# Weight pieces of 1024 columns for the high and low parts of an encoder's weights, on rings of four

## The chip, the cores and the metric

The kernel runs on one core of a Trainium2 chip. The metric is the device time of one execution in microseconds (us): the median of three runs. One more execution was recorded by the hardware profiler, and it has a time of its own. The profiler's names for the engines are PE (TensorE, the matrix engine; PEld is its loading of the stationary operand), DVE (VectorE), ACT (ScalarE), POOL (GpSimd) and SP (SyncE, which here only starts transfers).

## What is computed

An encoder trunk of two layers on 512 tokens of 1024 channels, all in fp32. Each layer modulates its input with a vector worked out from `c`, projects it with `w_in` into queries, keys, values and gates, runs two kinds of attention side by side, merges and projects them with `w_out`, and then sends each token through two of 16 experts:

```python
def _moe(h, w_router, router_bias, w_gate, w_up, w_down):
    ...
    hg = jnp.einsum('td,edf->tef', t, w_gate)
    hu = jnp.einsum('td,edf->tef', t, w_up)
    act = jax.nn.silu(hg) * hu * combine[..., None].astype(t.dtype)
    y = jnp.einsum('tef,efd->td', act, w_down)
    return y.reshape(b, s, d)

def reference(x, c, w_ada, ...):
    for l in range(DEPTH):
        ...
        h = _layer_norm(x) * (1.0 + sc1) + sh1
        mix = _mixer(h, w_in[l], ...)
        x = _layer_norm(DN_ALPHA * x + g1 * mix, ln1_g[l], ln1_b[l])
        h = _layer_norm(x) * (1.0 + sc2) + sh2
        ffn = _moe(h, w_router, router_bias, w_exp_gate[l], w_exp_up[l], w_exp_down[l])
        x = _layer_norm(DN_ALPHA * x + g2 * ffn, ln2_g[l], ln2_b[l])
    return x
```

An expert's gate and up weights are 1024 x 256, its down weights 256 x 1024. The kernel computes an expert only for the tokens that chose it, up to 128 of them.

## The kernel before

**Splitting the weights.** Nearly all products with weights are made from three matmuls in a faster 32-bit format. An operand is split into a high part, its value rounded to that format (`wH`, `xH`, `eH`), and a low part, what is left of it (`wL`, `xL`, `eL`); high x high, high x low and low x high are added up in PSUM (`gemm3`, lines 220 to 227). For weights this is done by `wsplit` (line 197). `wraw` (line 187) loads a tile of up to 8 KB for each partition as it lies in memory: 128 rows x 8 row blocks x 256 columns for `w_in`, gate and up, 128 x 2 x 1024 for down. `wsplit` then cuts it into pieces of 512 columns (`h` row blocks), and makes for each piece the high part by a cast on ScalarE (line 215) and the low part by a subtraction on VectorE (line 216).

**Where the tiles lie.** The raw tiles come from a ring of four (`NRAW`, tag `raw`) and one of five (`NE8`, tag `e8`); some that are loaded ahead of the experts lie in free tiles of other pools (`f4`, `row`, in blocks of 1024 columns). `WPAT` says which ring each expert's tile takes. The high and the low parts have rings of six pieces of 2 KB each (`NWH`). A slot comes free when its last reader is done, and the next piece takes any slot that is free.

**The order of the work.** Every engine runs its instructions in a fixed order. A scheduler lays it down when the program is built, from the program's order, the dependences and the time at which it reckons each slot to be free. So a change in the size or number of the slots moves instructions on all engines, though no line that orders them is touched.

**The experts.** For each expert `e` the program issues `x_gate(e)`, `x_down(e - 1)`, `x_up(e)`, `x_split(e + 1)`. `x_load` fetches the 128 tokens of an expert (`xe`, by an indirect transfer on POOL's queue). `x_split` transposes them on TensorE (tile `tp`) and splits them in two halves of 512 columns, row blocks 0 to 3 and 4 to 7, into `xH` and `xL`. `x_gate` and `x_up` are 24 matmuls each; the silu of the gate product and its product with the up product are `ea`. `x_down` transposes `ea` (`eT`), splits it (`eH`, `eL`) and multiplies it with the down weights: the columns 0 to 511 of `w_down` in plain fp32 with `eT`, the columns 512 to 1023 split, as `DS` says (lines 1153 to 1163). The result times a row, `ye`, is sent to the tensor `y2` by an indirect transfer; for the last two experts it stays on the chip (`yk`). On TensorE the planned order in the long stretch is: down product of one expert, up product of the next, transposes, gate product of the one after that, and again.

**Around the experts.** While the router decides which token goes where, the tiles of the first experts are loaded in the order of `AHEADW`, the last ones of it (from `HOLD` on) on POOL's queue after the first fetch of tokens. After the experts eight loads of `y` bring `y2` back (line 1309, SP's queue), and line 1315 adds them to `x`; then the next layer's `w_in` pieces follow. The `w_ada` tiles (`araw`) for the next modulation share the `raw` ring.

## Time and profile before

| | us |
|---|---|
| median of 3 runs | 1373.92 (1373.52 to 1374.74) |
| the profiled execution, its own time | 1374.85 |
| span of that execution in the trace | 1373.1 |
| TensorE busy | 1262.8 |
| VectorE busy | 1031.9 |
| ScalarE busy | 704.5 |

The span is the time from the first to the last instruction of the trace; the execution's own time is 1.75 us longer, for what lies before and after. Busy is the sum of the durations on one engine, without what it waits. Matmuls are pipelined: 24 of them in a row start every 0.12 us, though each is shown with 0.28 us, so that for TensorE the starts say more than the durations.

### The profile page before, as it was taken

To read this page: it belongs to the slowest core of one execution; us is meant where nothing else is said; L and a number is where in the kernel's file an instruction comes from. 1 tells how busy PE (TensorE), PEld (TensorE's weight loads), DVE (VectorE), ACT (ScalarE), POOL (GpSimd) and SP (SyncE) were. 2 spreads that over 40 slices of the span, in tenths; PEclk is the share of its full clock that TensorE was granted. 3 is DMA by queue.
4 is the path that set the end of the run, shared out by engine and by line. 5 is a ranking of instruction groups with operands and counts; after the bars stand their busy time and mean duration, and the time that the engine had idled before them with its cause. 6 is when DMAs were issued, how large, how long until landed. Compare 5 with 4: busy or idle time off the path is not lost.

```text
span 1373.1 us, 21373 instructions
## 1 busy us (share of the span) xinstructions
PE 1262.8 (92%) x7925; PEld 1027.6 (75%) x7925; DVE 1031.9 (75%) x2104; ACT 704.5 (51%) x1460; POOL 157.5 (11%) x161
## 2 busy tenths in 40 slices
PE   4898999999999949999969899999999994999996
PEld 3787777677778948888648777777777794788883
DVE  4877788776368879999886888564325978799997
ACT  2344444556644157777434454455556413777760
POOL 1032000000000222222020300000000012222210
PEclk9799999999999969999988999999999997899999
DMA  9747544455156187999643365112123546889963
GB/s 309 235 138 292 174 152 166 149 189 184 62 170 224 59 303 261 311 336 342 249 157 131 114 224 177 46 60 70 50 77 111 179 156 218 274 281 342 351 221 136
DMA packets 181070, 263.59 MB, mean 192 GB/s; under 512 B 18281, under 2 KB 131337, under 8 KB 180960
## 3 DMA queue, kind: packets, MB, share of 16 engines
q1 hardware_dynamic: 157104, 221.27, 47.8%
q0 software_dynamic: 11456, 24.07, 5.0%
q10 hardware_dynamic: 12400, 16.83, 3.8%
q8 instruction: 64, 1.05, 0.3%
q14 instruction: 46, 0.38, 0.1%
HBM read 250.79 MB, written 27.30 MB: 203 GB/s over the span
## 4 chain that ended last, share of the span: by engine, by line
PE 32%; DVE 10%; ACT 2%; issue 2%; DMA 2%; POOL 1%; SPq 1%; POOLq 0%; DVEq 0%; ACTq 0%
PE mm L225 5%; PE mm L226 5%; PE mm L227 5%; DVE wL L216 5%; PE mm L1188 3%; PE tp L330 2%; PE av L668 1%; PE y L1321 1%; ACT wH L215 1%; POOL rs L286 1%; PE mo L226 1%; PE mo L227 1%; PE mo L225 1%; PE s L634 1%; DMA raw<-in_w_exp_down 1%
## 5 line engine op out<-in xcount | busy, mean ns | idle before, releaser
L216 DVE TENSOR_TENSOR wL<-raw,wH 128x512 fp32r<-128x512 f32 x520 | 339.7, 685 | 94.4 <-ACT wH L215 80.6
L215 ACT CAST wH<-raw 128x512 fp32r<-128x512 f32 x520 | 318.4, 622 | 163.5 <-PE mm L1188 45.9
L225 PE MATMUL mm<-hH,wH 128*128 128x512 f32 x544 | 219.3, 403 | 0.0
L226 PE MATMUL mm<-hL,wH 128*128 128x512 f32 x544 | 217.9, 400 | 0.0
L227 PE MATMUL mm<-hH,wL 128*128 128x512 f32 x544 | 216.1, 397 | 0.0
L225 PE MATMUL mm<-wH,xH 128*128 128x256 f32 x512 | 149.1, 291 | 2.6 <-DVE yk L1189 1.6
L227 PE MATMUL mm<-wH,xL 128*128 128x256 f32 x512 | 148.6, 290 | 1.0 <-DVE xL L338 1.0
L226 PE MATMUL mm<-wL,xH 128*128 128x256 f32 x512 | 146.4, 286 | 0.3 <-DVE wL L216 0.3
L226 PEld LDWEIGHTS mm<-hL,wH 128*128 128x128 f32 x544 | 103.4, 190 | 21.9 <-issue 2.1
L225 PEld LDWEIGHTS mm<-hH,wH 128*128 128x128 f32 x544 | 103.2, 190 | 21.8 <-issue 0.8
L227 PEld LDWEIGHTS mm<-hH,wL 128*128 128x128 f32 x544 | 103.4, 190 | 21.2 <-issue 0.7
L249 DVE SCALAR_TENSOR_TENSOR acc<-araw,cond,acc 128x512 f32<-128x512 f32 x148 | 110.5, 747 | 5.7 <-DMA araw<-in_w_ada 3.0
L225 PEld LDWEIGHTS mm<-wH,xH 128*128 128x128 f32 x512 | 98.8, 193 | 5.5 <-DVE yk L1189 2.5
L226 PEld LDWEIGHTS mm<-wL,xH 128*128 128x128 f32 x512 | 98.6, 193 | 2.4 <-DVE wL L216 1.2
L227 PEld LDWEIGHTS mm<-wH,xL 128*128 128x128 f32 x512 | 98.2, 192 | 2.3 <-DVE xL L338 1.8
L286 POOL TENSOR_TENSOR rstd<-rstd,c_mhalf 128x1 f32<-128x1 f32 x32 | 20.4, 637 | 478.1 <-DVE rstd L285 478.1
L642 ACT ACTIVATE pp<-s,nm,rs 128x512 f32<-128x512 f32 x64 | 49.7, 778 | 33.0 <-DVE nm L639 31.3
L1188 PE MATMUL mm<-raw,eT 128*128 128x512 f32 x128 | 63.3, 617 | 3.6 <-ACT eT L1171 1.5
L225 PE MATMUL mm<-wH,hH 128*128 128x256 f32 x192 | 58.7, 308 | 5.4 <-ACT hH L406 3.6
L227 PE MATMUL mm<-wH,hL 128*128 128x256 f32 x192 | 57.2, 303 | 1.6 <-DVE hL L372 1.4
L1193 POOL DMA_INDIRECT y<-ye,vt x28 | 33.6, 1199 | 210.1 <-DVE ye L1189 210.1
L226 PE MATMUL mm<-wL,hH 128*128 128x256 f32 x192 | 56.7, 299 | 0.0
(303 smaller groups left out, 2655.7 us busy)
## 6 DMA issues: line engine op xcount, KB each, us to landing
araw<-in_w_ada SPq DMA_DIRECT2D x44, 1024.0 KB, 5.4
raw<-in_w_in SPq DMA_DIRECT2D x40, 1024.0 KB, 5.1
raw<-in_w_exp_gate SPq DMA_DIRECT2D x32, 1024.0 KB, 9.1
raw<-in_w_exp_up SPq DMA_DIRECT2D x28, 1024.0 KB, 11.1
raw<-in_w_exp_down SPq DMA_DIRECT2D x28, 1024.0 KB, 9.4
raw<-in_w_out SPq DMA_DIRECT2D x8, 1024.0 KB, 5.3
y<-y SPq DMA_DIRECT2D x16, 512.0 KB, 8.1
eraw<-in_w_ada SPq DMA_DIRECT2D x4, 1024.0 KB, 13.8
```

Source lines behind the costliest of these rows:

```text
L215: ACT.copy(H, raw(s))
L216: V.tensor_sub(L, raw(s), H.bitcast(F32))
L225: PE.matmul(o, lhsT=lH, rhs=rH, start=(i == 0), stop=False)
L226: PE.matmul(o, lhsT=lH, rhs=rL, start=False, stop=False)
L227: PE.matmul(o, lhsT=lL, rhs=rH, start=False, stop=(i == n - 1))
L249: last = V.scalar_tensor_tensor(acc, raw[:, k, :], ck, acc, op0=OP.mult, op1=OP.add)
L286: PO.tensor_tensor(r, r, mhalf[:, :n], op=OP.pow)
L330: return PE.transpose(dst, src, ident[0:k, 0:k])
L634: PE.matmul(s, lhsT=qT[h // 4][:, h % 4, tcols(t)], rhs=kTH[:, kv, :], start=True, stop=False)
L642: ACT.activation(pp, s, AF.Exp, bias=nm, scale=rs, accum_out=dn)
L1188: PE.matmul(p, lhsT=a, rhs=w, start=(i == 0), stop=(i == len(todo) - 1))
L1193: st = PO.indirect_dma_start(out=y2, out_offset=bass.IndirectOffsetOnAxis(ap=vidx[:, e:e + 1], axis=0), in_=ye, in_offset=None, bounds_che ...
```

## The change

`wsplit` cuts pieces of 1024 columns instead of 512. The rings of the high and low parts have four slots of 4 KB instead of six of 2 KB, and pay for it with one raw tile: three instead of four. A raw tile is now an object `Raw` that knows how many of its row blocks lie in one tile, so that a piece that crosses two blocks of an `f4` or `row` tile is filled by two instructions. The split half of the down weights is now one piece of 2 x 512 columns instead of two pieces of 512. An expert has five pieces instead of ten. Which tiles take which ring, and what is loaded ahead, is written anew for three raw tiles (`WPAT`, `AHEADW`, the tags in the first stage). `overflow`, which runs only if an expert has more than 128 tokens, is fitted to the new tiles.

```diff
--- before.py
+++ after.py
@@ -85,6 +85,13 @@
     return np.ascontiguousarray(np.concatenate(parts, 1))
 
 
+class Raw:
+
+
+    def __init__(self, at, n):
+        self.at, self.n = at, n
+
+
 def build(tc, A, out):
     nc = tc.nc
     with ExitStack() as es:
@@ -187,16 +194,16 @@
                 raws = [(fp if tag == "f4" else rp).tile([P, n] + shape[1:], F32, tag=tag, name="raw4") for _ in range(shape[0] // n)]
                 for i, raw in enumerate(raws):
                     eng.dma_start(raw, src[:, i * n:(i + 1) * n])
-                return lambda s: raws[s.start // n][:, s.start % n:s.start % n + s.stop - s.start]
+                return Raw(lambda s: raws[s.start // n][:, s.start % n:s.start % n + s.stop - s.start], n)
             raw = wp.tile([P] + shape, F32, tag="raw", name="raw", bufs=NRAW) if tag == "raw" else e8("raw8", shape)
             eng.dma_start(raw, src)
-            return lambda s: raw[:, s]
+            return Raw(lambda s: raw[:, s], shape[0])
 
         def wsplit(src, shape, big=False, tag="raw", behind=()):
 
-            raw = src if callable(src) else wraw(src, shape, tag)
+            raw = src if isinstance(src, Raw) else wraw(src, shape, tag)
             a = shape[0]
-            h = 512 // shape[1] if shape[1] < 512 else 1
+            h = min(a, 1024 // shape[1])
             hs = []
             if big:
                 h = a // 2
@@ -212,8 +219,11 @@
                 with ExitStack() as order:
                     for z in behind:
                         order.enter_context(tc.issue_after(z.ins))
-                    ACT.copy(H, raw(s))
-                    V.tensor_sub(L, raw(s), H.bitcast(F32))
+                    n = min(h, raw.n)
+                    for j in range(0, h, n):
+                        u, z = slice(j, j + n), raw.at(slice(i * h + j, i * h + j + n))
+                        ACT.copy(H[:, u], z)
+                        V.tensor_sub(L[:, u], z, H[:, u].bitcast(F32))
                 hs.append((H, L))
             return lambda k, c: tuple(z[:, k % h, c] for z in hs[k // h])
 
@@ -350,7 +360,7 @@
                     transposes(lambda i: xt[t][:, (4 * q + i) * P:(4 * q + i + 1) * P], p, 4)
                     for j in range(2):
                         (ACT.copy if j else V.tensor_copy)(zT[2 * q + j][:, :, tcols(t)], p[:, 2 * j:2 * j + 2, :])
-            tags = ["raw"] * 4 + ["e8"] * 4
+            tags = ["raw"] * 3 + ["e8"] * 5
             prev = None
             for c in (2, 3, 0, 1):
                 raw = ada_raw(0, c, 0, 4, tags.pop(0))
@@ -1150,18 +1160,10 @@
                 XS.pop(e)
                 V.tensor_mul(a, a, p)
                 raw = x_src(e, "down")
-                if not callable(raw):
+                if not isinstance(raw, Raw):
                     raw = wraw(raw, x_shape("down"), tags[e, "down"])
-                W = {}
-                for j in range(2):
-                    for k in range(2):
-                        w = raw(slice(k, k + 1))[:, :, 512 * j:512 * j + 512]
-                        if (k, j) in DS:
-                            w = wsplit(lambda s: w, [1, 512], behind=[order1] if e < 2 else [])
-                            W[k, j] = w(0, slice(0, 512))
-                        else:
-                            W[k, j] = w[:, 0]
-                WD[e] = a, W
+                Ws = wsplit(Raw(lambda s: raw.at(s)[:, :, 512:], raw.n), [2, 512], behind=[order1] if e < 2 else [])
+                WD[e] = a, {(k, j): Ws(k, slice(0, 512)) if j else raw.at(slice(k, k + 1))[:, 0, 0:512] for j in range(2) for k in range(2)}
 
             def x_down(e):
                 a, W = WD.pop(e)
@@ -1236,15 +1238,15 @@
                         def blocks(w, tags, view):
                             r = []
                             for i, tag in enumerate(tags):
-                                z = wp.tile([P, 512], F32, tag=tag, name="f" + w, bufs=NWH)
+                                z = wp.tile([P, 1024], F32, tag=tag, name="f" + w, bufs=NWH)
                                 ACT.dma_start(*view(z, A["w_exp_" + w][l][bass.ds(e, 1)], i))
                                 r.append(z)
                             return r
 
-                        pair = lambda z, a, i: (z.rearrange("p (k n) -> p k n", k=2),
-                                                a[:, 256 * i:256 * i + 256].rearrange("o (k p) n -> p (o k) n", p=P))
-                        fg = blocks("gate", ["wH"] * 4, pair)
-                        fu = blocks("up", ["wL"] * 4, pair)
+                        four = lambda z, a, i: (z.rearrange("p (k n) -> p k n", k=4),
+                                                a[:, 512 * i:512 * i + 512].rearrange("o (k p) n -> p (o k) n", p=P))
+                        fg = blocks("gate", ["wH"] * 2, four)
+                        fu = blocks("up", ["wL"] * 2, four)
                         fd = [f4(f"fd{k}", [D]) for k in range(2)]
                         for k in range(2):
                             ACT.dma_start(fd[k], A["w_exp_down"][l][bass.ds(e, 1)][0, P * k:P * k + P])
@@ -1260,7 +1262,7 @@
                             pu = pmm([P, 256])
                             for q, w in ((pg, fg), (pu, fu)):
                                 for k in range(8):
-                                    PE.matmul(q, lhsT=xT[:, k, :], rhs=w[k // 2][:, 256 * (k % 2):256 * (k % 2) + 256], start=(k == 0), stop=(k == 7))
+                                    PE.matmul(q, lhsT=xT[:, k, :], rhs=w[k // 4][:, 256 * (k % 4):256 * (k % 4) + 256], start=(k == 0), stop=(k == 7))
                             a = sc("fa", [256])
                             ACT.activation(a, pg, AF.Silu)
                             V.tensor_mul(a, a, pu)
@@ -1372,22 +1374,21 @@
 FDV = (0, 1, 4)
 BEHIND = ((0, "gate"), (0, "up"))
 HOLD = 10
-DS = ((0, 1), (1, 1))
-WPAT = ("e8",) * 5 + ("raw",) * 4
+WPAT = ("raw",) * 3 + ("e8",) * 5
 NE8 = 5
 NROW = 5
 SPLIT = ((1, 1, 0, 2), (1, 1, 0, 2))
 EKEEP = 2
 OPAT = (1, 3)
 NKEEP = 2
-NRAW = 4
-AHEADW = ((0, "gate", "raw"), (0, "up", "raw"), (0, "down", "raw"), (1, "gate", "raw"), (1, "up", "f4"), (1, "down", "f4"),
-          (2, "gate", "e8"), (2, "up", "e8"), (2, "down", "e8"), (3, "gate", "e8"), (3, "up", "e8"), (3, "down", "row"))
+NRAW = 3
+AHEADW = ((0, "gate", "raw"), (0, "up", "raw"), (0, "down", "raw"), (1, "gate", "e8"), (1, "up", "f4"), (1, "down", "f4"),
+          (2, "gate", "e8"), (2, "up", "e8"), (2, "down", "e8"), (3, "gate", "e8"), (3, "up", "row"))
 RLAG = 1
 AHEAD = 2
 NPE = 3
 ADA = ((4, 5, 8, 9, 6, 7, 10, 11, 14, 15, 12, 13, 16, 17), (8, 9, 6, 7, 10, 11))
-NWH = 6
+NWH = 4
 
 _INS = ["x", "c", "w_ada", "b_ada", "w_in", "q_norm_g", "k_norm_g", "w_branch_a", "w_branch_b", "w_out",
         "ln1_g", "ln1_b", "w_router", "router_bias", "w_exp_gate", "w_exp_up", "w_exp_down", "ln2_g", "ln2_b"]
```

The diff does not touch the order, but the scheduler lays down another one. Three places:

**VectorE, one expert of layer 1**, from its first gate piece on. Before; `raw_13412` is the gate tile, `raw_13482` the up tile of the same expert, `xL_13394` its tokens (`tp_13402` is their second half), `ea` belongs to the expert ahead of it:

```order
L216 TENSOR_TENSOR wL_13415<-raw_13412,wH_13414 128x512
L216 TENSOR_TENSOR wL_13419<-raw_13412,wH_13418 128x512
L1151 TENSOR_TENSOR ea_13312<-ea_13312,mm_13357 128x256
L216 TENSOR_TENSOR wL_13423<-raw_13412,wH_13422 128x512
L338 TENSOR_TENSOR xL_13394<-tp_13402,xH_13393 128x512
L216 TENSOR_TENSOR wL_13427<-raw_13412,wH_13426 128x512
L216 TENSOR_TENSOR wL_13485<-raw_13482,wH_13484 128x512
L216 TENSOR_TENSOR wL_13489<-raw_13482,wH_13488 128x512
L216 TENSOR_TENSOR wL_13493<-raw_13482,wH_13492 128x512
```

After; `raw_12869` is the gate tile, `raw_12931` the up tile of that expert, `xL_12851` its tokens (`tp_12859` their second half):

```order
L226 TENSOR_TENSOR wL_12872<-raw_12869,wH_12871 128x1024
L226 TENSOR_TENSOR wL_12876<-raw_12869,wH_12875 128x1024
L1161 TENSOR_TENSOR ea_12781<-ea_12781,mm_12818 128x256
L226 TENSOR_TENSOR wL_12934<-raw_12931,wH_12933 128x1024
L348 TENSOR_TENSOR xL_12851<-tp_12859,xH_12850 128x512
L226 TENSOR_TENSOR wL_12938<-raw_12931,wH_12937 128x1024
L348 TENSOR_TENSOR eL_12912<-tp_12906,eH_12911 128x256
L226 TENSOR_TENSOR wL_12970<-raw8_12967,wH_12969 128x1024
```

The second half of `xL` stood behind the third of four gate pieces; now both gate pieces are ahead of `ea`, and the first half of the up tile stands between `ea` and the second half of `xL`.

**ScalarE, the same two places.** Before, casts of `raw_13412` (gate) and then the second half of `xH_13393`, and casts of the up tile `raw_13482` behind it:

```order
L215 CAST wH_13414<-raw_13412 128x512
L215 CAST wH_13418<-raw_13412 128x512
L215 CAST wH_13422<-raw_13412 128x512
L215 CAST wH_13426<-raw_13412 128x512
L337 CAST xH_13393<-tp_13402 128x512
L215 CAST wH_13484<-raw_13482 128x512
L215 CAST wH_13488<-raw_13482 128x512
L215 CAST wH_13492<-raw_13482 128x512
L1144 ACTIVATE ea_13455<-mm_13430 128x256
```

After, the same with `raw_12869` (gate), `raw_12931` (up) and `xH_12850`:

```order
L225 CAST wH_12871<-raw_12869 128x1024
L225 CAST wH_12875<-raw_12869 128x1024
L225 CAST wH_12933<-raw_12931 128x1024
L347 CAST xH_12850<-tp_12859 128x512
L225 CAST wH_12937<-raw_12931 128x1024
L1154 ACTIVATE ea_12904<-mm_12879 128x256
```

The first cast of the up tile now stands ahead of the second half of `xH`. Expert 3 of each layer goes further: there the first up piece stands ahead of both halves of `xL`.

**SP's queue between the layers.** Before:

```order
L192 DMA raw<-in_w_exp_gate 128x8x256
L192 DMA raw<-in_w_exp_up 128x8x256
L192 DMA raw<-in_w_exp_down 128x2x1024
L1309 DMA y<-y_125 128x1024 x8
L192 DMA raw<-in_w_in 128x8x256 x4
L239 DMA araw<-in_w_ada 128x4x512
```

After:

```order
L199 DMA raw<-in_w_exp_gate 128x8x256
L199 DMA raw_6805<-in_w_exp_up 128x8x256
L199 DMA raw_6841<-in_w_exp_down 128x2x1024
L199 DMA raw<-in_w_in 128x8x256 x2
L1311 DMA y<-y_125 128x1024 x8
L199 DMA raw<-in_w_in 128x8x256 x2
```

Two of the four `w_in` loads of the next layer have moved from behind the eight `y` loads to ahead of them.

## Rows read from the trace of the kernel before

**Rows 1.** Page, part 1: engine, busy us, share of the span, instructions.

```profile
PE 1262.8 (92%) x7925; PEld 1027.6 (75%) x7925; DVE 1031.9 (75%) x2104; ACT 704.5 (51%) x1460; POOL 157.5 (11%) x161
```

**Rows 2.** Window: length, busy us of PE, PEld, DVE, ACT, POOL, clock, DMA share, GB/s.

```profile
175.00:400.00 225.00, 224.41 (x1379) 173.05 (x1376) 150.99 (x322) 119.08 (x291) 2.02 (x4) 1.00 0.46 150
525.00:660.00 135.00, 133.61 (x883) 113.95 (x882) 124.17 (x215) 103.72 (x196) 29.90 (x24) 1.00 0.90 302
1172.00:1325.00 153.00, 150.60 (x991) 129.02 (x991) 139.27 (x242) 117.48 (x221) 31.76 (x26) 0.99 0.89 301
```

**Rows 3.** The same columns, one expert (11 and 12 of layer 1) a row.

```profile
1217.49:1227.85 10.36, 10.28 (x68) 8.80 (x68) 9.53 (x17) 8.00 (x16) 2.54 (x2) 1.00 0.78 246
1227.85:1238.21 10.36, 10.28 (x68) 8.79 (x68) 9.53 (x17) 8.00 (x16) 2.54 (x2) 1.00 1.02 345
```

**Rows 4.** Groups by shape: busy us, mean ns of one, idle before.

```profile
L216 DVE TENSOR_TENSOR wL<-raw,wH 128x512 fp32r<-128x512 f32 x520 | 339.7, 685 | 94.4 <-ACT wH L215 80.6 <-PE tp L330 3.8 <-DVEq L1222 2.1
L215 ACT CAST wH<-raw 128x512 fp32r<-128x512 f32 x520 | 318.4, 622 | 163.5 <-PE mm L1188 45.9 <-DMA raw<-in_w_in 31.4 <-PE mm L226 29.9
...
L216 DVE TENSOR_TENSOR wLb<-raw,wHb 128x1024 fp32r<-128x1024 f32 x8 | 9.6, 1217 | 1.0 <-ACT wHb L215 1.0
...
L215 ACT CAST wHb<-raw 128x1024 fp32r<-128x1024 f32 x8 | 8.1, 1041 | 1.7 <-DMA raw<-in_w_out 1.7
```

**Rows 5.** Timeline of TensorE in that expert: start us, duration us.

```profile
1233.82 0.28 PE L227 MATMUL mm<-wH,xL 128*128 128x256 f32 x1
...
1234.62 0.28 PE L227 MATMUL mm<-wH,xL 128*128 128x256 f32 x1
...
1236.04 0.37 PE L227 MATMUL mm<-wH,xL 128*128 128x256 f32 x1
...
1237.20 0.28 PE L227 MATMUL mm<-wH,xL 128*128 128x256 f32 x1
```

**Rows 6.** Timeline of VectorE, same expert.

```profile
1234.24 0.41 DVE L1151 TENSOR_TENSOR ea<-ea,mm 128x256 f32<-128x256 f32 x1
1234.57 0.69 DVE L216 TENSOR_TENSOR wL<-raw,wH 128x512 fp32r<-128x512 f32 x1
1235.28 0.69 DVE L338 TENSOR_TENSOR xL<-tp,xH 128x512 fp32r<-128x512 f32 x1
```

**Rows 7.** Timeline of ScalarE, same expert.

```profile
1234.66 0.58 ACT L337 CAST xH<-tp 128x512 fp32r<-128x512 f32 x1
...
1237.51 0.38 ACT L1144 ACTIVATE ea<-mm 128x256 f32<-128x256 f32 x1
1237.79 0.37 ACT L1171 COPY eT<-tp 128x256 f32<-128x256 f32 x1
```

**Rows 8.** Timelines of SP's queue, VectorE, ScalarE between the layers.

```profile
665.00 7.33 SPq L1309 DMA_DIRECT2D y<-y  x8
...
669.31 1.28 DVE L1315 SCALAR_TENSOR_TENSOR x<-y,rt_gt,x 128x1024 f32<-128x1024 f32 x1 [0.84 <-DMA y<-y]
...
674.42 0.42 DVE L1151 TENSOR_TENSOR ea<-ea,mm 128x256 f32<-128x256 f32 x1 [0.24 <-PE mm L227]
...
688.08 2.50 DVE L216 TENSOR_TENSOR wL<-raw,wH 128x512 fp32r<-128x512 f32 x4 [2.98 <-ACT wH L215]
...
687.43 2.18 ACT L215 CAST wH<-raw 128x512 fp32r<-128x512 f32 x4 [11.28 <-DMA raw<-in_w_in]
```

**Rows 9.** Timelines of TensorE, GpSimd, ScalarE's queue before layer 1's experts.

```profile
1168.85 1.94 PE L330 MATMUL tp<-c_ident,xe 128*128 128x128 f32 x8 [6.76 <-DMA xe<-h2d,vt]
...
1164.22 1.16 POOL L1119 DMA_INDIRECT xe<-h2d,vt  x1 [9.22 <-DVE rt_gt L1209]
...
1156.31 0.34 ACTq L996 DMA_DIRECT2D h2d<-h  x1
```

**Rows 10.** Waits of TensorE by releaser: us in total, times, longest us.

```profile
PE tp L278 <- DVE mc L273: 3.6, 1, 3.6
...
PE mo L225 <- DVE mix L972: 2.1, 2, 1.0
...
PE mm L227 <- DVE xL L338: 1.0, 2, 0.5
```

## The prediction

> **What bounds the kernel now.** I read the page's first part, then busy time by stage, then one expert engine by engine, then the two seams of the program. The page gives TensorE 92% of the span and VectorE 75% [rows 1]. By stage the picture splits [rows 2]: attention in layer 0 (175 to 400) leaves TensorE nothing to win (224.41 of 225 us), and of the long expert stretches of the two layers (525 to 660, 1172 to 1325) it is idle only 135.00 - 133.61 = 1.39 and 153.00 - 150.60 = 2.40 us. One expert takes 10.36 us, with TensorE at 10.28 and VectorE at 9.53 [rows 3]. So TensorE sets the pace there, with VectorE close behind: about 0.8 us per expert is all that may be added to VectorE's work, and less than that if it is added at a bad place.
>
> The bad place is visible in one expert [rows 5 to 7]. TensorE runs a down product, an up product (24 matmuls, the last at 1233.82), four transposes, and then the next gate product (24 matmuls, up to 1237.20). A gate product needs the activations xH/xL in two halves: the first half for row blocks 0 to 3, the second for 4 to 7. The second half of xL is made by VectorE from 1235.28 to 1235.97, and the matmul that needs it, listed at 1236.04, takes 0.37 instead of 0.28 us: it already comes just in time, 0.09 us late. Ahead of it on VectorE stand ea (1234.24), which waits for the up product, and one piece of the gate weights (0.69 us).
>
> **What the split costs.** A piece of 128x512 costs VectorE 0.685 and ScalarE 0.622 us, one of 128x1024 1.217 and 1.041 us [rows 4]. Two small for one large save 0.153 us on VectorE and 0.203 us on ScalarE. 520 small pieces become 260 large ones (a few are filled by two half-size instructions): 260 x 0.153 = 40 us off VectorE, 53 us off ScalarE. Of this almost all lies beside TensorE's work, so it is worth little by itself: it pays only where TensorE waits for VectorE. Such waits are 3.6 us for mc at the start and 2.1 us for mix in the two joins [rows 10]. In each join some seven small subtractions precede the wait, seven halves of 0.153 or 0.5 us; at the start VectorE has perhaps ten pairs ahead, 1.5 us, and the waits that are smaller and not shown give about another 1.5 us. Together **-4 us** (0 to -7).
>
> **What the order costs in the experts.** The order of the new kernel puts the first up piece of the same expert ahead of the second half of xL on VectorE, and its cast ahead of the second half of xH on ScalarE; before, a gate piece of 512 stood there. With rings of four, the cast of this up piece takes the place of the previous expert's second up piece, which comes free with that product's last matmul. That makes a chain, in the times of the expert shown:
> - last up matmul 1233.82 + 0.28 = 1234.10; ea shows that a follower starts 0.14 us behind it, 1234.24 [rows 5, 6];
> - cast of the up piece on ScalarE, 1.041: 1235.28 [rows 4];
> - its subtraction on VectorE, 1.217: 1236.50;
> - second half of xL, 0.02 between the two and 0.69: 1237.21, against 1235.97 [rows 6].
>
> The matmul that waits for it therefore moves by 1.24 us; instructions in a row overlap by up to a tenth, so I take 1.15. The second half of xH, behind the cast, ends near 1235.28 + 0.58 = 1235.86 [rows 7], about when it is needed, and costs nothing further. Nothing gives the 1.15 us back: the nine or ten matmuls behind the wait, the silu on ScalarE that follows the last of them (1237.51), the copy of the transposed ea behind that (1237.79) and the next down product all follow at the old distances [rows 5, 7]. That the transposes of ea now stand ahead of the wait saves nothing, since the down product waits for ScalarE's copy behind the silu, not for them. The chain recurs with every expert, as two experts side by side have the same length [rows 3]. Experts 4 to 15 in both layers have this order: 24 x 1.15 = **+27.6 us**. Expert 3 has both halves of xL behind the up piece, so its gate product can go on only at about 1237.37 instead of 1234.62: 2.75 us, less the 0.09 of today, 2.6 each, **+5 us** for the two layers.
>
> The lower bound of the term is the VectorE chain alone, as if the slot were free early: ea ends at 1234.65, the piece and xL add 1.217 + 0.69, 1236.56, so 0.59 later than now; 24 x 0.55 + 2 x 2 = 17 us. The upper is 24 x 1.24 + 5.5 = 35 us.
>
> In the Trainium skill, the page Perfetto Trace Analysis, section Optimizing Scalar/DVE Operations, has two rules that point opposite ways here: larger operations help when the engine is saturated, and breaking instructions up lets work be done sooner when the engine isn't saturated but makes others wait. VectorE at 9.53 of 10.36 us is not the saturated engine in the experts [rows 3], so the second rule is the one that bears, and it speaks against the change; the first makes the rival below.
>
> **The seam between the layers.** The first two w_in loads now stand ahead of the eight y loads on SP's queue. Before, the y loads were issued from 665.00 on and the first add of y ran at 669.31, 4.3 us behind; the w_in loads came after them, so ScalarE waited 11.28 us for the first (687.43) and VectorE 2.98 us (688.08) [rows 8]. Now the second w_in load must wait for a raw tile (three instead of four), the one that the down weights of expert 14 hold until its product is half done, about 669; the y loads are queued behind it and land near 675. VectorE's first add of y stands ahead of yk of expert 14 and of ea of expert 15 (674.42), so all this moves by about 6 us. What comes back is the 2.98 us of waiting and up to 2.5 us of subtractions, which can go earlier. Net **+2 us**, from 0 (all of it refunded) to +5.
>
> **The router.** While the experts' first tokens are fetched TensorE waits 6.76 us (1168.85); the fetch goes out at 1164.22, after the write of h2d that was issued at 1156.31 [rows 9]. The new list of loads ahead puts one more 1 MB tile on SP's queue before that. At the 345 GB/s of the experts [rows 3] that is about 3 us of transfer, of which most is done before the write goes out: +1 us per layer (0 to 2.8). Against it, the gate pieces of expert 0 are now all cut before the tokens come: -0.5. For both layers **+1 us**.
>
> **Sum.** 27.6 + 5 + 2 + 1 - 4 = +31.6 us. The profiled execution took 1374.85 us, 0.93 above the median of the runs, so against the median 1373.92: about **1406 us**. All low ends together are +9, all high ends +45 us; they hardly fall together, so the likeliest case runs from 1387 to 1413.
>
> **Rivals.**
> - *The larger pieces win.* VectorE is the second limit, and five pairs less per expert are 0.77 us. If the up piece were cut before the gate product reaches its middle, the waits inside the experts (1.39 + 2.40 us) would shrink to nearly none and 4 us would be won outside, against 3 us at the seam and the router: 1374 - 5 = 1369. This is what the first of the two rules of the Trainium skill's Perfetto Trace Analysis (Optimizing Scalar/DVE Operations) would give. It decides from one point: the cast of the up piece must be over by 1234.0, so that its subtraction ends by 1235.3. For it: VectorE is at 92% of the expert. Against it: the slot isn't free until 1234.10. Chance 0.14, 1366 to 1371.
> - *Nothing that can be told.* The experts stay at 10.36 us, and the relief and the two seams cancel: 1372 to 1376. It needs the same early slot as the first rival. Chance 0.06. About 0.2%, 2.7 us, is what a measurement of this kernel can tell from no change.
> - *The loads become late.* Eight rotating weight tiles instead of nine. In the experts the DMA engines are busy 1.02 of their time at 345 GB/s [rows 3]. Three tiles of 1.05 MB are 9.1 us at that rate, below 10.36 and further below the 11.5 that I expect, so a slower expert makes this rarer. If it does happen, half a microsecond for each expert comes on top: 1418. Chance 0.06.
> - *The likeliest*, 0.74, of which some 0.06 lies below 1387 (the chain only partly exposed).
>
> Slower is then 0.74 + 0.06 = 0.80, same 0.06, faster 0.14. A range from 1372 to 1413 leaves out the faster case, 0.14, and most of the late loads, 0.05.
>
> **What would show it.** In the profile after: windows of one expert at 11.4 to 11.6 us; a single matmul L237 (wH, xL) in the middle of each gate product with about 1.1 us of idle time before it, released by VectorE's xL; the up piece's cast starting right behind the last up matmul. In the page, TensorE's idle time waiting for xL near 27 us instead of 1.0 [rows 10]. At the seam the first add of y near 6 us later relative to the last experts. The prediction is wrong if the expert keeps 10.36 us, or if the wait is there but the next down product doesn't move with it. The sum then loses its largest term, and the first two rivals are left.

## The result and the profile after

The changed kernel takes **1406.49 us** (1405.2 to 1409.66, 4 runs) against 1374.12 us of the kernel before in the same comparison: a ratio of 1.0246, 95% interval 1.0233 to 1.0259. It is slower by 32 us. (The ratios further down, too, are to the kernel before in the comparison of that run.) The forecast was 1406 us, a range from 1372 to 1413, and a chance of 0.80 for slower. The profiled execution has a span of 1403.4 us, 30.3 more than before.

The first line of the page (engine, busy us, share of the span, instructions), which answers to [rows 1]:

```profile
PE 1271.9 (91%) x7925; PEld 1030.6 (73%) x7925; DVE 1004.6 (72%) x1846; ACT 662.2 (47%) x1202; POOL 145.3 (10%) x159
```

VectorE has 258 instructions less and 1031.9 - 1004.6 = 27 us less to do, ScalarE 42 us less, and the kernel is slower all the same. TensorE runs as many matmuls as before. Two experts of the long stretch (window, busy us of PE, PEld, DVE, ACT, POOL, clock, DMA share, GB/s), to be held against [rows 3]:

```profile
1235.21:1246.78 11.57, 10.59 (x68) 8.80 (x69) 9.14 (x11) 7.04 (x11) 2.21 (x2) 1.00 0.94 314
1246.78:1258.35 11.57, 10.59 (x69) 8.80 (x69) 9.14 (x11) 7.04 (x11) 2.20 (x2) 1.00 0.97 327
```

An expert takes 11.57 us instead of 10.36, with less work on VectorE (9.14 instead of 9.53) and on ScalarE (7.04 instead of 8.00). Two rows of the list of TensorE's waits (us in total, times, longest) show where it now waits in the experts:

```profile
PE mm L237 <- DVE xL L348: 18.5, 28, 0.9
...
PE mm L1190 <- ACT eT L1173: 9.3, 26, 0.7
```

The wait for xL, 1.0 us in all before [rows 10], is 18.5 us, 28 times. The second row is the next down product, which waits for ScalarE's copy of the transposed ea.

The timeline of TensorE in the expert of the first window (start us, duration us; what it waited stands in brackets), to be held against [rows 5]:

```profile
1243.41 0.28 PE L236 MATMUL mm<-wL,xH 128*128 128x256 f32 x1
1243.53 0.38 PE L340 MATMUL tp<-c_ident,ea 128*128 128x128 f32 x2
1244.58 0.39 PE L237 MATMUL mm<-wH,xL 128*128 128x256 f32 x1 [0.67 <-DVE xL L348]
...
1245.76 0.28 PE L237 MATMUL mm<-wH,xL 128*128 128x256 f32 x1
...
1246.78 1.98 PE L1190 MATMUL mm<-raw,eT 128*128 128x512 f32 x4 [0.30 <-ACT eT L1173]
```

Two matmuls in a row start 0.12 us apart. Between the matmul at 1243.41 and the next one at 1244.58 there are 1.17 us; the transposes of ea fill a part of them, so the list counts only 0.67 as idle. The next down product waits 0.30 us, but that adds nothing: from the last gate matmul to it there are 1.02 us (1245.76 to 1246.78), before 1.01 (1237.20 to 1238.21), and the transposes of ea stood there then. VectorE in the same stretch, against [rows 6]:

```profile
1242.38 0.41 DVE L1161 TENSOR_TENSOR ea<-ea,mm 128x256 f32<-128x256 f32 x1
1242.71 1.22 DVE L226 TENSOR_TENSOR wL<-raw,wH 128x1024 fp32r<-128x1024 f32 x1
1243.84 0.68 DVE L348 TENSOR_TENSOR xL<-tp,xH 128x512 fp32r<-128x512 f32 x1
```

and ScalarE, against [rows 7]:

```profile
1241.60 1.05 ACT L225 CAST wH<-raw 128x1024 fp32r<-128x1024 f32 x1 [0.40 <-PE mm L237]
1242.55 0.58 ACT L347 CAST xH<-tp 128x512 fp32r<-128x512 f32 x1
```

The cast of the up piece runs from 1241.60 to 1242.65, 0.03 us behind the end of the last up matmul (1241.28 + 0.29 in the same timeline). The subtraction of that piece starts at 1242.71, right behind the cast; but ea, ahead of it on VectorE, runs from 1242.38 to 1242.79, and the next instruction starts some 0.08 before such an end, here as in the kernel before [rows 6]. So both ways to the subtraction are equally long. Then xL starts at 1243.84, and the matmul runs at 1244.58.

**Where the 30 us are.** The same instructions in both timelines of TensorE divide the program. Before: the first pos matmul of layer 0, the down product of experts 0, 14 and 15, the last y matmuls, the first pos matmul and the first down product of layer 1:

```profile
495.39 0.17 PE L1066 MATMUL pos<-asgb,trib 128*128 128x16 bf16 x1 [9.34 <-DVE asgb L1058]
...
520.28 1.98 PE L1188 MATMUL mm<-raw,eT 128*128 128x512 f32 x4
...
667.01 1.98 PE L1188 MATMUL mm<-raw,eT 128*128 128x512 f32 x4 [0.52 <-ACT eT L1171]
...
676.16 1.88 PE L1188 MATMUL mm<-raw,eT 128*128 128x512 f32 x4
...
706.12 1.88 PE L1321 MATMUL y<-yk,G 128*128 128x512 f32 x4
...
1159.00 0.17 PE L1066 MATMUL pos<-asgb,trib 128*128 128x16 bf16 x1 [9.39 <-DVE asgb L1058]
...
1184.73 1.98 PE L1188 MATMUL mm<-raw,eT 128*128 128x512 f32 x4
```

After, the same seven places:

```profile
499.10 0.17 PE L1076 MATMUL pos<-asgb,trib 128*128 128x16 bf16 x1 [9.35 <-DVE asgb L1068]
...
525.75 1.98 PE L1190 MATMUL mm<-raw,eT 128*128 128x512 f32 x4 [0.63 <-ACT eT L1173]
...
689.82 1.98 PE L1190 MATMUL mm<-raw,eT 128*128 128x512 f32 x4 [0.74 <-ACT eT L1173]
...
699.54 1.88 PE L1190 MATMUL mm<-raw,eT 128*128 128x512 f32 x4
...
723.46 1.88 PE L1323 MATMUL y<-yk,G 128*128 128x512 f32 x4
...
1171.02 0.17 PE L1076 MATMUL pos<-asgb,trib 128*128 128x16 bf16 x1 [9.38 <-DVE asgb L1068]
...
1198.37 1.98 PE L1190 MATMUL mm<-raw,eT 128*128 128x512 f32 x4 [0.63 <-ACT eT L1173]
```

| stretch | before | after | difference | forecast |
|---|---|---|---|---|
| start to pos of layer 0 | 495.39 | 499.10 | +3.7 | } -4 |
| pos of layer 1, counted from the last y of layer 0 | 452.88 | 447.56 | -5.3 | } |
| pos to the first down product, both layers | 50.62 | 54.00 | +3.4 | +1 |
| down products of experts 0 to 2 (here the tokens of expert 3 are split), both layers | 44.8 | 50.6 | +5.7 | +5 |
| down products of experts 2 to 15, both layers | 266.9 | 295.9 | +29.0 | +27.6 |
| last down product to last y matmul, layer 0 | 29.96 | 23.92 | -6.0 | +2 |
| the same and the end, layer 1 | 32.5 | 32.3 | -0.2 | 0 |
| sum | | | +30.3 | +31.6 |

The large term came as forecast. Most of the small ones did not; that the sums agree within 1.3 us is luck, since their errors cancel. Each column is one execution: the three kernels that differ only in `WPAT` (before, experiments 5 and 8) have the first pos matmul at 495.39, 495.64 and 495.13, so a few tenths of a us in a row say nothing.

### The profile page after: what moved, and what is told of

It is laid out like the page before. It is cut to its first block, busy times and chain, and to the rows that moved or that the text cites. A ratio compares the mean times of both kernels' runs of the same rounds, so it can differ in the third digit from the quotient of the medians.

```text
span 1403.4 us, 20612 instructions
## 1 busy us (share of the span) xinstructions
PE 1271.9 (91%) x7925; PEld 1030.6 (73%) x7925; DVE 1004.6 (72%) x1846; ACT 662.2 (47%) x1202; POOL 145.3 (10%) x159
## 3 DMA queue, kind: packets, MB, share of 16 engines
q8 instruction: 64, 1.05, 0.3%
## 4 chain that ended last, share of the span: by engine, by line
PE 34%; DVE 7%; ACT 3%; issue 3%; DMA 2%; POOL 1%; ACTq 0%; POOLq 0%; DVEq 0%; SPq 0%
PE mm L237 6%; PE mm L235 6%; PE mm L236 6%; PE mm L1190 3%; PE tp L340 2%; DVE wL L226 2%; PE av L678 1%; ACT wH L225 1%; PE y L1323 1%; PE mo L236 1%; PE mo L235 1%; PE mo L237 1%; DMA araw<-in_w_ada 1%; DVE xL L348 1%; PE sB L724 1%
## 5 line engine op out<-in xcount | busy, mean ns | idle before, releaser
L226 DVE TENSOR_TENSOR wL<-raw,wH 128x1024 fp32r<-128x1024 f32 (+1 forms) x262 | 317.2, 1216 | 107.3 <-ACT wH L225 104.4
L225 ACT CAST wH<-raw 128x1024 fp32r<-128x1024 f32 (+1 forms) x262 | 271.5, 1045 | 176.3 <-PE mm L1190 56.1
L237 PE MATMUL mm<-wH,xL 128*128 128x256 f32 x512 | 149.5, 292 | 18.5 <-DVE xL L348 18.5
L235 PE MATMUL mm<-wH,xH 128*128 128x256 f32 x512 | 154.6, 302 | 4.3 <-ACT wH L225 2.0
L259 DVE SCALAR_TENSOR_TENSOR acc<-araw,cond,acc 128x512 f32<-128x512 f32 x144 | 107.2, 744 | 5.4 <-DMA araw<-in_w_ada 3.9
L340 PE MATMUL tp<-c_ident,xe 128*128 128x128 f32 x256 | 43.3, 281 | 13.2 <-DMA xe<-h2d,vt 13.2
```

The lines of the kernel that those rows point to most:

```text
L225: ACT.copy(H[:, u], z)
L226: V.tensor_sub(L[:, u], z, H[:, u].bitcast(F32))
L235: PE.matmul(o, lhsT=lH, rhs=rH, start=(i == 0), stop=False)
L237: PE.matmul(o, lhsT=lL, rhs=rH, start=False, stop=(i == n - 1))
L259: last = V.scalar_tensor_tensor(acc, raw[:, k, :], ck, acc, op0=OP.mult, op1=OP.add)
L340: return PE.transpose(dst, src, ident[0:k, 0:k])
```

## Experiments

**Theory and rivals.** The theory: the up piece that stands ahead of the second half of xL costs what its slot's lateness, its cast and its subtraction add, and the rest follows. Rival one: rings of four slots are too short, whatever the order. Rival two: three raw tiles make the loads late. The first four kernels tell these apart.

**1. The order put back, on both engines.** `x_split` keeps its two instructions for the second half, and an up piece is placed behind them:

```diff
+                    hi = ACT.copy(xH[:, 4 * q:4 * q + 4, :], p)
+                    lo = V.tensor_sub(xL[:, 4 * q:4 * q + 4, :], p, xH[:, 4 * q:4 * q + 4, :].bitcast(F32))
+                XM[e] = [hi, lo]
...
-                W = wsplit(..., behind=[order1] if (e, w) in BEHIND else [])
+                W = wsplit(..., behind=([order1] if (e, w) in BEHIND else []) + (XM[e] if w == "up" else []))
```

> The changed kernel with one thing put back: on ScalarE and on VectorE every up piece is ordered behind the second half of the same expert's xH and xL. Pieces of 1024, rings of four and three raw tiles stay. If the up piece ahead of xL is the cause, the expert goes back from 11.57 to 10.3 to 10.4 us, the wait for xL in the gate product is gone, and the time falls by 24 x 1.2 + 5 = about 34 us, to 1371 to 1375 us. Rival: the rings of four are too short whatever the order, so the next wait (the up piece, cut later) takes the place of this one; then the expert stays above 11.2 us and the time above 1397 us. Rival: loads come late on three raw tiles; then the time stays near 1406 us.

Measured: 1375.15 us, 1.0016 of before (1.0001 to 1.0031), and 10.45 us for an expert. One expert (the columns of [rows 3]), and VectorE in it:

```profile
1238.76:1249.20 10.44, 10.36 (x68) 8.77 (x68) 9.21 (x12) 6.93 (x11) 2.21 (x2) 1.00 1.01 347
...
1245.94 0.41 DVE L1163 TENSOR_TENSOR ea<-ea,mm 128x256 f32<-128x256 f32 x1
1246.27 0.68 DVE L1142 TENSOR_TENSOR xL<-tp,xH 128x512 fp32r<-128x512 f32 x1
1247.05 2.36 DVE L226 TENSOR_TENSOR wL<-raw,wH 128x1024 fp32r<-128x1024 f32 x2
```

xL now follows ea at once, and the two up pieces come behind it. Some 31 us come back with the same pieces, the same rings and the same three raw tiles, so the loss hangs on this order, and rivals one and two fall. (That it takes large pieces as well is shown by experiments 3 and 4.) A rest of 0.09 us for each expert stays; its cause was not followed up.

**2. The order put back on VectorE only.**

```diff
-                XM[e] = [hi, lo]
+                XM[e] = [lo]
```

> As the run before, but only VectorE's order is put back: xL stands ahead of the up piece's subtraction, while on ScalarE the up piece's cast still stands ahead of xH. By the chain, xH is ready at 1242.55 + 0.58 = 1243.13 and xL 0.69 later, at 1243.85 instead of 1244.52: the expert falls by 0.67 us to 10.9 us, the time by 24 x 0.67 = 16 us to about 1390 us. If the subtraction on VectorE alone were the cause, it would be as fast as with both orders put back (10.36 us, 1373 us); if the cast alone were, nothing would change (11.57 us, 1406 us).

Measured: 1387.13 us (1.0103, 1.0068 to 1.0137), 10.89 us for an expert. ScalarE and VectorE in one of them:

```profile
1243.47 1.05 ACT L225 CAST wH<-raw 128x1024 fp32r<-128x1024 f32 x1 [0.35 <-PE mm L237]
1244.43 0.58 ACT L1141 CAST xH<-tp 128x512 fp32r<-128x512 f32 x1
...
1245.04 0.69 DVE L1142 TENSOR_TENSOR xL<-tp,xH 128x512 fp32r<-128x512 f32 x1 [0.32 <-ACT xH L1141]
```

The cast still stands ahead of xH on ScalarE; xH ends at 1245.01 and xL starts at 1245.04. VectorE had done ea before and waited 0.32 us. So of the 1.12 us between the two ends (11.57 and 10.45), the cast ahead of xH costs 0.44 by itself, and the subtraction ahead of xL adds 0.68 to it. The other half, ScalarE's order put back and VectorE's not, was not run.

**3. Small pieces on the rest of the change.** The kernel before with three raw tiles, the new `WPAT` and `AHEADW` and the new tags of the start, and `NWH = 8` slots of 512 columns:

```diff
-NRAW = 4
+NRAW = 3
...
-NWH = 6
+NWH = 8
```

> The kernel before with the rest of the change only: pieces of 512 columns stay, on rings of eight slots of 2 KB; raw ring of three, the new rings for the experts' tiles and the new list of loads ahead. Here too the up piece stands ahead of xL, but it is a small one and its slot is free early. If size and slot make the price, the expert stays at 10.36 to 10.45 us and the time is that of before but for the seams, 1370 to 1380 us. If the raw tiles and the loads were the cause, the expert is at 11.5 us and the time above 1400 us; if the mere order were, the expert is near 11 us.

Measured: 1370.13 us (0.9979, 0.9962 to 0.9996). The down products of two experts that follow each other start 10.35 us apart:

```profile
1235.28 1.98 PE L1188 MATMUL mm<-raw,eT 128*128 128x512 f32 x4
...
1245.63 1.98 PE L1188 MATMUL mm<-raw,eT 128*128 128x512 f32 x4
```

Here too a piece of the up tile stands ahead of xL, but a small one whose slot is free early. So it isn't the name of the piece that costs; the price is its size and its slot. The same run has the late start (pos at 499.78) and the fast seam (25.57 us) of the changed kernel, which thus don't come from the large pieces.

**4. Large slots, small instructions.** Each slot of 4 KB is filled by two casts and two subtractions:

```diff
-                    n = min(h, raw.n)
+                    n = min(h, raw.n, max(1, 512 // shape[1]))
```

> The changed kernel with its slots of 4 KB on rings of four, but each slot filled by two casts and two subtractions of 512 columns. The slot comes free as late as in the changed kernel, only what stands between ea and xL is halved: cast 0.62 from 1234.24, subtraction 0.685, xL 0.69 end at 1236.25 instead of 1237.21 in the times of the kernel before. The expert should then take 10.6 us (10.5 to 10.8), the time 1380 to 1388 us. If the lateness of the slot were all of it and the size nothing, the expert would stay at 11.3 us or more.

Measured: 1377.4 us (1.0039, 1.0023 to 1.0055), below the 1380 to 1388 that were expected; 10.58 us for an expert, as expected. VectorE:

```profile
1244.26 0.42 DVE L1161 TENSOR_TENSOR ea<-ea,mm 128x256 f32<-128x256 f32 x1
1244.59 0.68 DVE L226 TENSOR_TENSOR wL<-raw,wH 128x512 fp32r<-128x512 f32 x1
1245.19 0.68 DVE L348 TENSOR_TENSOR xL<-tp,xH 128x512 fp32r<-128x512 f32 x1
```

Only half of the up piece stands between ea and xL, 0.60 instead of 1.13 us from start to start. Of the 1.21 us, 0.99 go with the size of the instruction. The 0.22 that stay go with the slots: experiment 3, with the same order on VectorE and instructions of the same size on slots of 2 KB, takes 10.35. Between the pos matmuls and the first down product it takes 24.57 and 24.16 us instead of 26.65 and 27.35: the loss there goes with the size of the instructions, too, in part by way of TensorE's clock (see the router below).

**5. The seam: two w_in loads ahead of the y loads, in the kernel before.** One line decides which ring the experts' tiles take, and with it when the raw tiles come free:

```diff
-WPAT = ("e8",) * 5 + ("raw",) * 4
+WPAT = ("raw",) * 2 + ("e8",) * 5 + ("raw",) * 2
```

> The kernel before with one line changed: WPAT begins with two raw tiles, then five e8, then two raw. Pieces of 512, rings of six, four raw tiles and the list of loads ahead are as before. By this, two w_in loads of the next layer come to stand ahead of the eight y loads, as in the changed kernel. If this order made the 6 us that the seam gained there (29.96 to 23.92 us from the last down product to the last y matmul) and the 5 us behind it (452.9 to 447.6), they come here too, with the experts at 10.36 us and the start as before: 1362 to 1366 us against about 1373. If the gain came from the pieces or from the ring of three, this kernel is within 2 us of before.

Measured: 1369.05 us, 0.9973 of before (0.9962 to 0.9984): faster than both kernels. From the last down product to the last y matmul it takes 23.19 us instead of 29.96. The first line is the matmul that waited 5.99 us in the kernel before; then SP's queue and the same matmul in this run:

```profile
694.01 3.59 PE L1321 MATMUL y<-yk,G 128*128 128x512 f32 x4 [5.99 <-DVE rstd L285]
...
648.13 4.12 SPq L192 DMA_DIRECT2D raw<-in_w_in  x2
665.36 5.74 SPq L1309 DMA_DIRECT2D y<-y  x8
...
689.93 1.98 PE L1321 MATMUL y<-yk,G 128*128 128x512 f32 x4 [1.70 <-DVE rstd L285]
```

Two w_in loads go out at 648.13, and the y loads at 665.36, as before [rows 8]. ScalarE no longer waits for w_in, and TensorE's wait behind it is 1.70 us. Behind that matmul, too, it is faster: up to the last y matmul it takes 10.50 us, with a granted clock of 1.00, and 12.11 before (694.01 to 706.12), with 0.87. (1.00 is 2.4 GHz throughout; below it, a part of the time is at 1.2.) So 1.6 of the 6.8 us are TensorE's clock, which in the kernel before is lower behind the wait of 5.99 us. The 5 us of the stretch behind the seam did not come (452.65 against 452.88): that part of the expectation was wrong, and this is why the time is above 1366.

**6. The seam the other way: y first, in the changed kernel.**

```diff
+            with ExitStack() as order:
+                for z in YLAST[:l]:
+                    order.enter_context(tc.issue_after(z.ins))
                 return wsplit(A["w_in"][l]...)
```

> The changed kernel with one thing put back: all w_in loads of the second layer stand behind the eight y loads again. If the order of these loads made the gain at the seam, it goes: the stretch from the last down product to the last y matmul is again near 30 us instead of 23.9, the time 1411 to 1416 us. My prediction had said that the new order costs 2 us; by that the time would fall to 1404 us.

Measured: 1409.71 us (1.0269, 1.0253 to 1.0286), some 3 us above the changed kernel, though the two intervals meet. SP's queue:

```profile
686.64 4.17 SPq L1316 DMA_DIRECT2D y<-y  x8
694.53 16.15 SPq L199 DMA_DIRECT2D raw<-in_w_in  x4
```

The stretch takes 26.84 us instead of 23.92, not the 30 that were expected, and the step from expert 14's to expert 15's down product 8.67 instead of 9.72. Both together are 1.9 us longer, not 6. Even of these only 0.2 lie ahead of the matmul that waits for rstd (690.41 to 713.72 here, 689.82 to 712.95 in the changed kernel); behind it TensorE has a granted clock of 0.86 instead of 1.00. So with large pieces the order itself is worth next to nothing; why it is worth more with small ones was not followed up.

**7. Four raw tiles, rings of three.**

```diff
-NRAW = 3
+NRAW = 4
...
-NWH = 4
+NWH = 3
```

> The changed kernel with four raw tiles again, and rings of three slots of 4 KB for the high and low parts, so that the memory is the same. If the ring of three raw tiles made the 3.7 us that the first layer lost ahead of its experts (its pos matmuls at 499.1 instead of 495.4), they are at 495 to 496 us here. In the experts a gate piece of 1024 stands between ea and xL; three slots let even fewer pieces be cut ahead, so the expert takes at least 10.9 us, more likely 11.5 to 12.5, and the time is 1390 to 1430 us. If the loss at the start came from the large pieces, it stays.

Measured: 1411.19 us (1.0283, 1.0266 to 1.0301), 11.57 us for an expert. Its first pos matmul:

```profile
492.05 0.17 PE L1076 MATMUL pos<-asgb,trib 128*128 128x16 bf16 x1 [9.38 <-DVE asgb L1068]
```

That is 7 us ahead of the changed kernel, and 3.3 ahead of the one before. So with large pieces three raw tiles with rings of four cost 7 us at the start against four with rings of three; with small ones the three raw tiles cost 4.4 (499.78 in experiment 3 against 495.39), and with four raw tiles the large pieces give 3.3. The expectation had been 495 to 496 us. In the experts the order is another one here: it is a gate piece of 1024 columns that stands between ea and xL. TensorE waits earlier, 0.51 us for a wL of the gate, but the matmul that needs xL comes as late, 3.31 us behind the last up matmul (1245.67 to 1248.98) against 3.30, and the expert takes the same 11.57 us. So it makes no difference which tile the large piece in that place is from.

**8. All four w_in loads ahead of y.** The kernel before with

```diff
-WPAT = ("e8",) * 5 + ("raw",) * 4
+WPAT = ("e8",) + ("raw",) * 4 + ("e8",) * 4
```

> The kernel before with WPAT one raw, ... four raw in the second to fifth place: now all four w_in loads stand ahead of the y loads. If ScalarE's and VectorE's wait for w_in is all that the order removes, this is as fast as two loads ahead, 1362 to 1366 us; if the y loads then come too late behind four transfers of 1 MB, the seam loses some 3 us for each further load, 1366 to 1372 us.

Measured: 1373.96 us (1.0008, 0.9993 to 1.0022), above both ranges that were expected. SP's queue, and VectorE's first add of y:

```profile
647.15 11.36 SPq L192 DMA_DIRECT2D raw<-in_w_in  x4
668.82 4.47 SPq L1309 DMA_DIRECT2D y<-y  x8
...
672.93 1.28 DVE L1315 SCALAR_TENSOR_TENSOR x<-y,rt_gt,x 128x1024 f32<-128x1024 f32 x1 [5.08 <-DMA y<-y]
```

The y loads go out at 668.82 instead of 665.00, and the add of y, ahead of yk on VectorE, waits 5.08 us; TensorE's step from expert 14 to 15 is 16.08 us instead of 9.15. This is the loss of 6 us that I had forecast for the changed kernel. It exists, but needs more loads ahead than two, and it takes back all that the order gives.

**9. Four raw tiles, rings of three, small instructions.** Experiment 7 with the halves of experiment 4 and the `WPAT` of experiment 5.

```diff
-NRAW = 3
+NRAW = 4
...
-NWH = 4
+NWH = 3
...
-                    n = min(h, raw.n)
+                    n = min(h, raw.n, max(1, 512 // shape[1]))
```

> Four raw tiles, rings of three slots of 4 KB, each slot filled by two casts and two subtractions of 512 columns; WPAT two raw, five e8, two raw. With four raw tiles and pieces of 1024 the first layer was 3.3 us faster up to its pos matmuls than the kernel before (492.05 against 495.39). If that came from fewer and larger instructions, it is gone here (495 to 496); if from the larger slots, which let more be cut ahead, it stays (492 to 493). In the experts a gate half of 512 stands between ea and xL, as in the kernel before: by the chain 10.36 to 10.6 us, and with one w_in load ahead of the y loads the time is 1364 to 1374 us. If three slots are too few, the expert is at 11 us or more and the time above 1385 us.

Measured: 1376.68 us (1.0012, 0.9992 to 1.0032), above the 1364 to 1374 that were expected; 10.57 us for an expert. The first pos matmul:

```profile
494.94 0.17 PE L1076 MATMUL pos<-asgb,trib 128*128 128x16 bf16 x1 [9.34 <-DVE asgb L1068]
```

The 3.3 us of experiment 7 are gone but for 0.45, about what kernels with the same start differ by: they belonged to the size of the instructions, not of the slots. Against experiment 4 (498.26, three raw tiles and rings of four, instructions of the same size) it is 3.3 us earlier.

## Why the prediction was right, and where it was not

**The experts: right, in place, mechanism and size.** The forecast was 1.15 us for each of 24 experts, from a slot that is free 0.14 us behind the last up matmul, a cast of 1.041, a subtraction of 1.217 and xL of 0.69. Measured are 1.21 for each, of which 1.08 lie between the last up matmul and the one that waits (1241.28 to 1244.58, before 1233.82 to 1236.04), where the forecast's 1.15 belongs; the cast takes 1.05, the subtraction 1.22, xL 0.68, and the slot is free at once (0.03 us). What I had as the lower bound, VectorE's own way through ea, is just as long in the changed kernel, since the second gate piece ends only at 1242.46 and pushes ea back: its cast, too, had to wait for a slot (it starts at 1240.15, 0.03 us behind the twelfth up matmul, the last to read the first up piece). So the two ways meet within 0.1 us, and taking away one of them (experiment 2) brings only the part that belongs to it. The waits in the list are shorter than forecast, 18.5 us for xL and not 27, because the transposes of ea fill a part. Experiments 1, 3 and 4 measure the order, the size and the slot one by one, and in each the expert lands within 0.1 us of what was expected of it. With that the rivals fall: the larger pieces did not win even with the order put back (experiment 1, 1.0016 of before); and late loads are excluded by experiment 1, which has the same raw tiles and the same loads at 10.45 us. By the rule of the Trainium skill that was cited (Perfetto Trace Analysis, Optimizing Scalar/DVE Operations, on engines that aren't saturated), smaller instructions may let the work be done sooner. This case's runs agree: 10.58 us for an expert with halves against 11.57.

**Expert 3: the size right, the reason only half of it.** The forecast was 2.6 us for a layer (its 1237.37 is 0.16 later than the chain that it is taken from, which ends at 1237.21). The step in which expert 3's gate product stands, from the second down product to the third, takes 12.95 us instead of 10.36 in both layers, 2.59 more; the step ahead of it 0.28 more. But with the order put back (experiment 1) it still takes 11.76: the order explains 1.19. What the forecast left out is that all eight transposes of expert 3's tokens now stand behind the up product, where four stood before (1202.86 in the timeline of before), so that the casts and subtractions of both halves come one after the other when TensorE already needs the first:

```profile
1216.78 1.03 PE L340 MATMUL tp<-c_ident,xe 128*128 128x128 f32 x8
...
1220.02 0.39 PE L237 MATMUL mm<-wH,xL 128*128 128x256 f32 x1 [0.95 <-DVE xL L348]
```

In experiment 3, with pieces of 512, seven of the eight stand there as well, and the step takes 11.96: this half doesn't come from the size of the pieces.

**The seam: wrong, by 8 us.** The step that failed is "the second w_in load must wait for a raw tile ... the one that the down weights of expert 14 hold until its product is half done". SP's queue in the changed kernel, and TensorE's wait that was 5.99 us before:

```profile
677.18 8.74 SPq L199 DMA_DIRECT2D raw<-in_w_in  x2
686.14 11.05 SPq L1311 DMA_DIRECT2D y<-y  x8
...
712.95 1.98 PE L1323 MATMUL y<-yk,G 128*128 128x512 f32 x4 [2.42 <-DVE rstd L295]
```

The two w_in loads are out by 685.92 and the y loads follow from 686.14, 3.7 us ahead of expert 14's down product (689.82), not 2 us behind its start. By `WPAT` the last three raw tiles are expert 14's up and down and expert 15's gate. The second load goes at 685.55 (issuing one takes 0.37 us), 0.03 behind the last subtraction of expert 15's gate (684.29 + 1.23): it took that tile, and never waited for the one of the down weights. So the 6 us of lateness did not come: the first add of y runs 3.1 us behind expert 14's down product (692.90), before 2.3. What I had counted as coming back did come, and more, 1.6 us of it by TensorE's clock as in experiment 5 (712.95 to 723.46 takes 10.51 us at 1.00, before 12.11 at 0.87). Experiments 5 and 8 show both sides of that scale: two loads ahead win 6 us, four lose them again.

**The router: forecast +1, measured +3.4.** The fetch of the tokens was not late, as I had it: from pos to the first transposes it takes 9.25 and 10.13 us, before 9.91 and 9.85. The loss lies behind it. In each layer TensorE waits 1.00 us for a large cast of expert 0's up tile (511.91 and 1184.71); with halves this wait is gone (experiment 4). That is 2.0 of the 3.4 us. The rest goes with TensorE's clock: from these transposes to those of the next expert the granted share is 0.63 and 0.64, before 0.76 and 0.68, in experiment 4 0.69 and 0.76.

**Start and second layer: forecast -4 for the relief, measured +3.7 and -5.3.** The work that the larger pieces save was put too high: VectorE has 27 us less to do and ScalarE 42, not 40 and 53. The mean durations were multiplied, but the small pieces overlap more: 520 of 0.685 make 356 us, and VectorE was busy with them for 339.7 [rows 4]. Still the waits that the term named, 3.6 us for mc and 2.1 for mix, are gone from the list after the change. At the start the step that failed is the one left out: the w_in tiles share the raw ring with the w_ada tiles, and one raw tile fewer costs 3.3 to 7 us (experiments 3, 4, 7 and 9; the rings differ by a slot or two in each pair). That it costs by this sharing is read from the program, and no run separates it. All five kernels with four raw tiles have their first pos matmul between 492.0 and 495.6, all six with three between 498.3 and 499.8. The relief by larger pieces, which I had at some 3 us there, is 3.3 us where four raw tiles are left (experiments 7, 9).

Of the 5.3 us of the second layer 3.4 are TensorE's clock, in the stretch from the last y matmul to the first matmul of the next modulation (`adap`). Before, and then after (the columns of [rows 3]):

```profile
706.12:789.68 83.56, 73.22 (x458) 65.71 (x456) 64.55 (x147) 40.99 (x99) 19.07 (x12) 0.90 0.33 111
...
723.46:803.65 80.19, 70.75 (x458) 63.40 (x456) 62.56 (x137) 38.82 (x89) 16.84 (x12) 0.94 0.34 116
```

83.56 us at 0.90 and 80.19 at 0.94 are the same 75 us of full clock, and the other kernels fit: experiment 4 takes 83.8 at 0.90, experiment 9 78.2 at 0.96. What sets the clock there was not tested, so these 3.4 us can't be put down to the change. The other 1.9 lie between there and the pos matmul, and go with the raw tiles: 369.3 to 369.7 us in the five kernels with four of them, 367.4 to 368.5 in the six with three. Why three are faster there stays open.

## What to carry to other kernels

Where an engine that isn't the bottleneck feeds one that is, look at what stands directly ahead of the operand that comes last: on an engine that runs in a fixed order, a larger instruction there can be paid nearly in full (here 1.21 us for an expert, 0.99 of it by the size), though it saves busy time everywhere else. Fewer, larger slots move instructions even if no line on the order is touched, so compare the planned order of both kernels at the place where the bottleneck has least room, and add up the chain from the release of the slot. A right sum of many terms proves at most its large one: here three small terms were off by 2 to 8 us and cancelled.

## What the runs showed of the hardware

Casts and subtractions in a row overlap: two of 1024 columns on VectorE take 2.36 us (1247.05 in experiment 1), not 2 x 1.217 = 2.43. A cast on ScalarE followed the release of its slot by TensorE after 0.03 us, less than the 0.14 us that I had taken from ea on VectorE (the ends of matmuls are modelled, so both are rough). TensorE's granted clock over the same stretch of the program differed between the kernels' profiles, 0.90 to 0.96 in the 80 us behind the seam and 0.63 to 0.76 at expert 0, and made more than 3 us of a stage; so look at the clock of a stage before its time is put down to a change. Executions of one kernel lay further apart than I had taken from the three runs shown: the kernel before ran in 1368.58 to 1376.81 us in 25 runs on one chip, 0.6%.
